# Keeping the written order of the matmuls in a hybrid encoder block's projections and second MLP product

## The chip, the cores and the metric

The kernel runs on one core of a Trainium2 chip. The metric is device time in microseconds (us) of one execution, lower is better. Three timed executions before the change took 2259.14, 2265.67 and 2268.3 us, so the median is 2265.67 us. One further execution was recorded by the hardware profiler. It took 2259.7 us, with a span from first to last instruction of 2257.9 us.

PE is the matrix engine (PEld its loading of the stationary operand), DVE, ACT and POOL are the vector, scalar and GpSimd engines, and SP issues the DMAs. PSUM is the memory into which PE accumulates, cut into banks of 128 x 512 float32.

## The reference

One layer on 2048 tokens, model width 1024, float32, one sequence:

```
mod = SiLU(c) W_ada + b_ada            -> shift, scale, gate for mixer and MLP
h   = RMSNorm(x) * (1 + scale) + shift
[xin | B | C | q | k | v | g] = h W_in           # 1024 -> 7 x 512
conv part  = B * causal_depthwise_conv3(C * xin)
retention  = chunked decay retention on rotary q, k, with v; per-head norm; SiLU(g) gate
x = x + gate  * RMSNorm(concat(conv, retention) W_out)
h = RMSNorm(x) * (1 + scale') + shift'
x = x + gate' * RMSNorm(relu(h W_1)^2 W_2)       # 1024 -> 4096 -> 1024
```

## The kernel before, in words

**A product in three parts.** Every float32 operand of the large products is split into a high and a low part (`hi`, `lo`) of a type that PE reads in one pass. ACT writes the high part, DVE the low part. The helper `mm3` then issues three matmuls into one PSUM bank: stationary high with moving high (line 141), stationary high with moving low (line 142), stationary low with moving high (line 143). The first two have the same stationary operand. All three are 128 x 128 by 128 x 512.

**The mixer.** The tokens go through in four blocks of 512. A block runs seven projections of `W_in` and two halves of `W_out`, as `gemm_nat` (tokens stationary, weights moving) or `gemm_t` (weights stationary, tokens moving). Each takes four banks, one for each 128 tokens or columns, and walks over eight steps of the inner dimension, at each step over the four banks, at each bank over the three parts. The weights come in groups of two steps through `wgroup`: one DMA of 512 KB into `raw`, an ACT copy to `whi` (line 135), a DVE subtraction to `wlo` (line 137), each with three buffers. The order of projections in a block is V, K, G, Q, XIN, then the retention (small products of 128 x 128 and 128 x 512 on the tiles `m`), CG, BG, the two halves of `W_out`. In block 0, V and three of the four banks of K are done in the start-up stage by calls of their own.

**Banks.** The pool `gp` has six banks for the names `g`, taken in turn; the pool `mp` has two for the names `m`. A projection's bank comes free when the engine that reads it is done with the projection that had the same bank six allocations earlier. For K and Q that reader is `rotary` on DVE (lines 529 and 538), which needs the tables of sines and cosines that `rope_tables` makes at the start of each block by a long row of small DVE operations (lines 361 to 397) and three ACT operations (lines 394 to 399).

**Between blocks** `h2_prep` transposes the finished block through the two `m` banks (line 480), with ACT and DVE reading them in turns (lines 484 to 486).

**The MLP.** Both products go by a scheme of seven products in place of eight on 2 x 2 blocks, for two halves B of the tokens. `fc1` has weights stationary (`wh`, `wl` from the pool `hp`) and prepared tokens moving (`qh`, `ql`). These tokens lie in the pools `hA` and `hB`, and for product number 4 in the tiles of the pool `tp`. Product 4 is the last of the seven of a step, except in the very first step. `fc2` walks, for each of the seven products, over 16 steps: it loads the step's stationary block from DRAM into the halves of a tile `f` (pool `late`, names `f`), the moving one into `wh`, `wl`, and calls `mm3` for four banks. The last six steps of the very last product are held in the pool `hB` first and then done bank by bank (`prod_held`).

**What sets the order.** The kernel is written as one program. A scheduler gives each engine its queue: it walks the program with a model of the instructions' times, and puts next on an engine what its model says can start first. The order of a queue is then fixed, and each engine works its queue in that order, waiting on semaphores for operands and free buffers. Between matmuls that accumulate into one bank with the flags of `mm3` the first must lead and the last must close; between banks nothing holds the written order.

Of the kernel before, what the change touches and what calls it, by code (L numbers as in the profile page):

```python
# [54 lines left out]
def block_kernel(  # L55
# [5 lines left out]
    nc = tc.nc  # L61
# [15 lines left out]
    def nm(s):  # L77
        n_of[s] = n_of.get(s, 0) + 1
        return f"{s}_{n_of[s]}"
# [13 lines left out]
    def bank(shape=(P, 512)):  # L93
        return gp.tile(list(shape), F32, tag="g", name=nm("g"))

    def mbank(shape=(P, 512)):
        return mp.tile(list(shape), F32, tag="m", name=nm("m"))
# [32 lines left out]
    def wgroup(src, eng=None, pool=None):  # L130
        pool, n = (wp, 3) if pool is None else (pool, 2)
        raw = pool.tile([P, 1024], F32, tag="raw", name=nm("raw"), bufs=n)
        nc.sync.dma_start(raw, src)
        hi = pool.tile([P, 1024], F32R, tag="whi", name=nm("whi"), bufs=n)
        nc.scalar.copy(hi, raw)  # L135
        lo = pool.tile([P, 1024], F32R, tag="wlo", name=nm("wlo"), bufs=n)
        (eng or nc.vector).tensor_tensor(lo, raw, hi.bitcast(F32), op=ALU.subtract)  # L137
        return hi, lo

    def mm3(ps, ah, al, bh, bl, first, last):  # L140
        nc.tensor.matmul(ps, ah, bh, start=first, stop=False)  # L141
        nc.tensor.matmul(ps, ah, bl, start=False, stop=False)  # L142
        nc.tensor.matmul(ps, al, bh, start=False, stop=last)  # L143

    ALL = list(range(NT))

    def gemm_nat(groups, lhs, ks, toks=ALL):

        bs = [bank() for _ in toks]
        n = 0  # L150
        for g, kp in zip(groups, ks):
            hi, lo = wgroup(g)
            for kk, k in enumerate(kp):
                c = slice(kk * 512, kk * 512 + 512)
                xh, xl = lhs[k]
                for ps, t in zip(bs, toks):
                    s = slice(t * P, t * P + P)
                    mm3(ps, xh[:, s], xl[:, s], hi[:, c], lo[:, c], n == 0, n == 2 * len(ks) - 1)
                n += 1
        return bs  # L160

    def gemm_t(groups, rhs):

        bs = [bank() for _ in range(4)]
        n = 0
        for kp, g in enumerate(groups):
            hi, lo = wgroup(g)
            for kk in range(2):
                k = 2 * kp + kk
                xh, xl = rhs[k]  # L170
                for j in range(4):
                    s = slice(kk * 512 + j * P, kk * 512 + j * P + P)
                    mm3(bs[j], hi[:, s], lo[:, s], xh, xl, n == 0, n == 2 * len(groups) - 1)
                n += 1
        return bs

# [10 lines left out]
    def mod1(kt):  # L187

        pt = st.tile([P, 256], F32, tag="pt", name=nm("pt"), bufs=4)
        for i in range(2):  # L190
            raw = st.tile([P, 4, 256], F32, tag="ada", name=nm("ada"), bufs=8)
            last = nc.sync.dma_start(raw, ada1[kt, i].rearrange("p (k c) -> p k c", k=4))
            for k in range(4):
                c_ = sc[:, 4 * i + k : 4 * i + k + 1]
                if i == k == 0:
                    nc.vector.tensor_scalar(pt, raw[:, k, :], c_, None, op0=ALU.mult)
                else:
                    nc.vector.scalar_tensor_tensor(  # L198
                        pt, raw[:, k, :], c_, pt, op0=ALU.mult, op1=ALU.add
                    )  # L200
        return pt, last
# [69 lines left out]
    with tc.tile_pool(name="st", bufs=NK) as st:  # L271
# [10 lines left out]
        ps = mbank()  # L282
# [28 lines left out]
        nxt, last = mod1(1)  # L311
        h0_tile(0, pts)
        start_ps = [bank() for _ in range(6)] + [extra]
        for k in range(NK):
            if k % 2 == 0 and k > 0:
                ws = startup_weights(k // 2)
            pts = nxt
            if k + 2 < NK:
                nxt, last = mod1(k + 2)
            c = slice(k % 2 * 512, k % 2 * 512 + 512)  # L320
            xh, xl = h_cur[k]
            for i, (w, t) in enumerate([(0, t) for t in range(NT)] + [(1, t) for t in range(3)]):
                if i == 2 and k + 1 < NK:
                    h0_tile(k + 1, pts)
                s = slice(t * P, t * P + P)
                hi, lo = ws[w]
                mm3(start_ps[i], xh[:, s], xl[:, s], hi[:, c], lo[:, c], k == 0, k == NK - 1)
# [5 lines left out]
    def at(tag, shape=(P, 512), dt=F32, bufs=4):  # L333
        pool = {"yh": pl, "yl": pl, "kT": late, "sg": late}.get(tag, pa)
        return pool.tile(list(shape), dt, tag=tag, name=nm(tag), bufs=bufs)
# [156 lines left out]
    NP = DFF // P // 2  # L492
# [21 lines left out]
    with pa_stack:  # L514
# [30 lines left out]
        for b in range(NB):  # L545

            if b == 0:
                vps, kps = start_ps[:NT], start_ps[NT:]
            else:
                vps = gemm_nat(w_in(VV), h_cur, KS)  # L550
# [22 lines left out]
            if b == 0:  # L573
                for t in range(3):
                    k_end(t, kps[t])
                k_end(3, gemm_nat(w_in(KK), h_cur, KS, ALL[3:])[0])
            else:
                for t, ps in enumerate(gemm_nat(w_in(KK), h_cur, KS)):
                    k_end(t, ps)
# [23 lines left out]
            for j, ps in enumerate(gemm_t(w_in(XIN), h_cur)):  # L603
                u = at("u", (P, TB + 2))
                nc.scalar.copy(u[:, 2:], ps)
                us.append(u)
# [11 lines left out]
            for t in range(NT):  # L618
                ps = mbank()
                for h in range(H):  # L620
                    s = slice(h * P, h * P + P)
# [4 lines left out]
                if b * NT + t < SEQ // P - 1:  # L626
                    ps = mbank()
                    for h in range(H):
                        s = slice(h * P, h * P + P)
# [4 lines left out]
                    else:  # L634
                        for h in range(H):
                            s = slice(h * P, h * P + P)
# [4 lines left out]
                for h in range(H):  # L641
                    s = slice(h * P, h * P + P)
# [21 lines left out]
            for j, ps in enumerate(gemm_t(w_in(CG), h_cur)):  # L664
                u = us[j]
                nc.vector.tensor_tensor(u[:, 2:], ps, u[:, 2:], op=ALU.mult)
                nc.gpsimd.tensor_copy(u[:, 0:2], halo[:, j, :])
                nc.gpsimd.tensor_copy(halo[:, j, :], u[:, TB : TB + 2])
                c_ = at("qT")
                nc.gpsimd.tensor_scalar(c_, u[:, 0:TB], cw[:, 0, j : j + 1], 1.0, op0=ALU.mult, op1=ALU.mult)  # L670
                for i in (1, 2):
                    nc.vector.scalar_tensor_tensor(
                        c_, u[:, i : i + TB], cw[:, i, j : j + 1], c_, op0=ALU.mult, op1=ALU.add
                    )
                cc.append(c_)
# [3 lines left out]
            for t in range(NT):  # L679
# [5 lines left out]
                for h in range(H):  # L685
                    s = slice(h * P, h * P + P)
# [10 lines left out]
            for j, ps in enumerate(gemm_t(w_in(BG), h_cur)):  # L697
                y = tmp()
                nc.vector.tensor_tensor(y, ps, cc[j], op=ALU.mult)
                nc.scalar.copy(yh[j], y)  # L700
                nc.vector.tensor_tensor(yl[j], y, yh[j].bitcast(F32), op=ALU.subtract)
# [9 lines left out]
            for ch, tag in enumerate(("kT", "sg")):  # L711
                ms = []
                for t, ps in enumerate(gemm_nat([wout[ch * 4 + k0 // 2] for k0, _ in ko], ys, ko)):
                    m = at(tag)
# [235 lines left out]
    def fc2(B, beside=None):  # L950
# [6 lines left out]
        def operands(i, t, pool=None):  # L957
            return split512(ld(fd[B][i][t]), held(pool) if pool else f_pair()) + split512(
                ld(right(i, t)), held(pool) if pool else w_
            )  # L960

        def prod(i, bs, upto=NP, aside=None):
            for t in range(upto):
                if beside is not None and i in (1, 2) and t % 4 == 2:
                    next(beside, None)
                ah, al, bh, bl = operands(i, t)
                for n, ps in enumerate(bs):
                    s = slice(n * P, n * P + P)
                    mm3(ps, ah[:, s], al[:, s], bh, bl, t == 0, t == NP - 1)
                if aside is not None:  # L970
                    next(aside, None)

# [35 lines left out]
        def whole(i, n):  # L1008
            prod(i, sets[n % 2])
            return sets[n % 2]  # L1010
# [36 lines left out]
        if B == 0:  # L1047
            prod(4, sets[0], NP, up)

            def lower():  # L1050
                for t in R:
                    last(t, nc.gpsimd)
                yield
                for t in R:
                    finish(1, t, (c21[t], c22[t]))
                    yield

            return lower()
        prod(4, sets[0], NP - 6, up)
        for t in prod_held(4, sets[0], NP - 6):  # L1060
            last(t, nc.vector)
# [94 lines left out]
```

## Time and profile before

| what | value |
|---|---|
| three timed executions | 2259.14, 2265.67, 2268.3 us |
| the profiled execution, its span | 2259.7 us, 2257.9 us |
| PE, PEld busy | 2162.3 us (96%), 1770.0 us (78%), 9736 instructions each |
| DVE, ACT, POOL busy | 1441.0, 981.0, 614.0 us |
| mean granted PE clock | 0.988 of full |
| start-up stage and first weights | up to about 88 us |
| mixer, four blocks | about 88 to 977 us |
| fc1, fc2 of the first half of the tokens | about 978 to 1300 us, 1300 to 1627 us |
| fc1, fc2 of the second half | about 1627 to 1932 us, 1932 to 2247 us |

A row of the timeline gives the start, the length, the engine, the line, the operation, the written tile, the read tiles (for a matmul the moving one, then the stationary one), the shape, the count, and in brackets the engine's idle time before it with what ended it. A matmul's length is that of its way through the array, and the next one starts before it ends; what a matmul costs is therefore the distance from its start to the next one's, called its pitch here. A row of the windows gives a stretch in us, its length, the busy time of PE with the matmuls that touch it, the granted clock, and DMA share and GB/s.

### The profile page before, as it was taken

The page shows a single profiled execution, that of the slowest core. Times are in us where ns is not written, and L with a number is a line of the kernel's source. Part 1 is how long each engine was busy: PE and PEld are TensorE (multiplying, and loading weights), DVE is VectorE, ACT ScalarE, POOL GpSimd, SP SyncE. Part 2 cuts the span into 40 slices and gives each one's busy share as a digit, 9 for nine tenths or more (in the row PEclk, how much of TensorE's full clock was granted, in tenths as well). Part 3 has the DMA queues.
Part 4 walks back from the last instruction along what each step waited for, and adds up shares of the span by engine and source line. Part 5 has one row for each costly group of instructions (what it writes and reads, how often), then busy time and mean ns, then how long its engine had stood idle before and what let it go on. Part 6 is the DMA issues. An engine that isn't in the chain of part 4 may idle for free.

```text
span 2257.9 us, 28832 instructions
## 1 busy us (share of the span) xinstructions
PE 2162.3 (96%) x9736; PEld 1770.0 (78%) x9736; DVE 1441.0 (64%) x2182; ACT 981.0 (43%) x1714; POOL 614.0 (27%) x457
## 2 busy tenths in 40 slices
PE   3999999999999999989999999999999999999997
PEld 3788777878777888868888877888788888888886
DVE  7766854774576535796666686555776666555557
ACT  3332532254224522565555555444455555444444
POOL 4133163305323442152333232001433333010012
PEclk8999999999999999999999999999999999999999
DMA  7456576446555563665444575666664444756556
GB/s 280 140 168 222 160 242 230 164 156 219 196 181 193 195 228 108 225 198 182 150 153 151 193 236 183 200 187 187 223 215 149 154 149 150 225 177 199 187 187 242
DMA packets 197429, 428.25 MB, mean 190 GB/s; under 512 B 22560, under 2 KB 22560, under 8 KB 197280
## 3 DMA queue, kind: packets, MB, share of 16 engines
q1 hardware_dynamic: 197280, 426.41, 56.8%
q8 instruction: 76, 1.25, 0.2%
q14 instruction: 73, 0.60, 0.1%
HBM read 322.51 MB, written 103.81 MB: 189 GB/s over the span
## 4 chain that ended last, share of the span: by engine, by line
PE 67%; issue 10%; DMA 9%; DVE 9%; POOL 3%; ACT 1%; SPq 0%; POOLq 0%; DVEq 0%; ACTq 0%
PE g L142 20%; PE g L143 20%; PE g L141 19%; DMA w2r<-in_w 2%; DMA w2d<-w2r 2%; PE m L142 2%; PE m L143 2%; PE m L141 2%; POOL w2r L501 2%; DMA ada<-in_ada 2%; DVE wlo L137 1%; DMA x<-in_x 1%; DVE wl L802 1%; DVE ql L802 1%; DVE pt L198 1%
## 5 line engine op out<-in xcount | busy, mean ns | idle before, releaser
L801 ACT CAST wh<-r 128x512 fp32r<-128x512 f32 x442 | 273.3, 618 | 220.3 <-PE g L142 203.5
L143 PE MATMUL g<-qh,wl 128*128 128x512 f32 x896 | 350.5, 392 | 7.6 <-DVE wl L802 7.6
L141 PE MATMUL g<-qh,wh 128*128 128x512 f32 x896 | 350.3, 391 | 1.8 <-ACT wh L801 1.8
L142 PE MATMUL g<-ql,wh 128*128 128x512 f32 x896 | 350.1, 391 | 0.0
L802 DVE TENSOR_TENSOR wl<-r,wh 128x512 fp32r<-128x512 f32 x442 | 321.1, 727 | 8.8 <-ACT wh L801 8.4
L802 DVE TENSOR_TENSOR f<-r,f 128x512 fp32r<-128x512 f32 x218 | 164.2, 753 | 229.0 <-ACT f L801 228.8
L135 ACT CAST whi<-raw 128x1024 fp32r<-128x1024 f32 x148 | 155.1, 1052 | 344.6 <-PE g L143 178.3
L860 DVE TENSOR_TENSOR q<-g,q 128x512 f32<-128x512 f32 x267 | 178.3, 686 | 185.6 <-PE g L143 183.3
L137 DVE TENSOR_TENSOR wlo<-raw,whi 128x1024 fp32r<-128x1024 f32 x140 | 188.1, 1347 | 149.2 <-ACT whi L135 148.8
L142 PE MATMUL g<-wl,f 128*128 128x512 f32 x680 | 271.1, 399 | 9.0 <-DVE wl L802 9.0
L801 ACT CAST f<-r 128x512 fp32r<-128x512 f32 x218 | 135.2, 620 | 311.3 <-PE m L143 149.5
L143 PE MATMUL g<-wh,f 128*128 128x512 f32 x680 | 268.5, 395 | 0.0
L143 PEld LDWEIGHTS g<-qh,wl 128*128 128x128 f32 x896 | 168.6, 188 | 44.7 <-DVE wl L802 9.0
L141 PEld LDWEIGHTS g<-qh,wh 128*128 128x128 f32 x896 | 168.6, 188 | 38.0 <-ACT wh L801 2.4
L141 PE MATMUL g<-wh,f 128*128 128x512 f32 x680 | 195.8, 396 | 1.3 <-ACT wh L801 1.3
L142 PEld LDWEIGHTS g<-ql,wh 128*128 128x128 f32 x896 | 168.6, 188 | 36.0
L987 POOL TENSOR_TENSOR q<-q,gg 128x512 f32<-128x512 f32 x28 | 42.0, 1523 | 484.9 <-ACT q L984 484.9
L142 PEld LDWEIGHTS g<-wl,f 128*128 128x128 f32 x680 | 128.5, 189 | 43.7 <-DVE wl L802 12.4
L878 POOL TENSOR_TENSOR r<-r,r 128x512 f32<-128x512 f32 x32 | 41.9, 1310 | 435.2 <-DVE wl L802 392.2
L141 PEld LDWEIGHTS g<-wh,f 128*128 128x128 f32 x680 | 128.3, 189 | 32.5 <-ACT wh L801 2.1
L143 PEld LDWEIGHTS g<-wh,f 128*128 128x128 f32 x680 | 128.5, 189 | 29.3
L141 PE MATMUL g<-whi,r 128*128 128x512 f32 x315 | 125.9, 405 | 12.5 <-DVE tmp L538 7.6
(253 smaller groups left out, 4218.5 us busy)
## 6 DMA issues: line engine op xcount, KB each, us to landing
raw<-in_win SPq DMA_DIRECT2D x116, 512.0 KB, 4.2
r<-in_w SPq DMA_DIRECT2D x224, 256.0 KB, 4.5
fd<-q SPq DMA_DIRECT2D x224, 256.0 KB, 2.2
r<-fd SPq DMA_DIRECT2D x224, 256.0 KB, 2.7
r<-w2d SPq DMA_DIRECT2D x128, 256.0 KB, 2.7
ada<-in_ada SPq DMA_DIRECT2D x48, 512.0 KB, 4.6
w2r<-in_w SPq DMA_DIRECT2D x32, 512.0 KB, 5.2
raw<-in_wout SPq DMA_DIRECT2D x32, 512.0 KB, 4.4
```

The costliest lines, as they stand in the source:

```text
L135: nc.scalar.copy(hi, raw)
L137: (eng or nc.vector).tensor_tensor(lo, raw, hi.bitcast(F32), op=ALU.subtract)
L141: nc.tensor.matmul(ps, ah, bh, start=first, stop=False)
L142: nc.tensor.matmul(ps, ah, bl, start=False, stop=False)
L143: nc.tensor.matmul(ps, al, bh, start=False, stop=last)
L198: nc.vector.scalar_tensor_tensor(pt, raw[:, k, :], c_, pt, op0=ALU.mult, op1=ALU.add)
L501: nc.gpsimd.tensor_tensor(o, a, b_, op=ALU.subtract)
L801: nc.scalar.copy(hi, src)
L802: nc.vector.tensor_tensor(lo, src, hi.bitcast(F32), op=SUB)
L860: (eng or nc.vector).tensor_tensor(o, a, b_, op=ADD)
L878: nc.gpsimd.tensor_tensor(b11, b12, b11, op=SUB)
L987: eng.tensor_tensor(c, c, gg[1][:, j * 512 : j * 512 + 512], op=ALU.mult)
```

## The change

`mm3` gets a name of a row. Matmuls that carry the same name are tied one behind the other, in the order in which they are written, by an ordering rule for the scheduler that adds no semaphore. Each projection (`gemm_nat`, and `gemm_t` in the same way as the diff shows for `gemm_nat`) is a row of its own, and all of `fc2` of one half of the tokens is one row, without the held last steps. The matmuls of the start-up stage and of `fc1` get no row. Two rows are free against each other, and so are all other instructions. No instruction is added or removed. Behind the change the three matmuls stand in lines 159 to 161, and other lines 20 further down.

```diff
+    def behind(a, b):
+        tc.add_manual_dep(
+            a.ins, b.ins.name,
+            mybir.DependencyInfo(mybir.DependencyClass.NoSync, mybir.DependencyReason.DATA),
+            reason="order",
+        )
+    row_of = {}
+    def in_row(row, m):
+        if row is not None:
+            if row in row_of:
+                behind(m, row_of[row])
+            row_of[row] = m
-    def mm3(ps, ah, al, bh, bl, first, last):
-        nc.tensor.matmul(ps, ah, bh, start=first, stop=False)
-        nc.tensor.matmul(ps, ah, bl, start=False, stop=False)
-        nc.tensor.matmul(ps, al, bh, start=False, stop=last)
+    def mm3(ps, ah, al, bh, bl, first, last, row=None):
+        in_row(row, nc.tensor.matmul(ps, ah, bh, start=first, stop=False))
+        in_row(row, nc.tensor.matmul(ps, ah, bl, start=False, stop=False))
+        in_row(row, nc.tensor.matmul(ps, al, bh, start=False, stop=last))
...
     def gemm_nat(groups, lhs, ks, toks=ALL):
         bs = [bank() for _ in toks]
+        row = nm("row")
...
-                    mm3(ps, xh[:, s], xl[:, s], hi[:, c], lo[:, c], n == 0, n == 2 * len(ks) - 1)
+                    mm3(ps, xh[:, s], xl[:, s], hi[:, c], lo[:, c], n == 0, n == 2 * len(ks) - 1, row)
...
-                    mm3(ps, ah[:, s], al[:, s], bh, bl, t == 0, t == NP - 1)
+                    mm3(ps, ah[:, s], al[:, s], bh, bl, t == 0, t == NP - 1, f"fc2_{B}")
```

The scheduler's result is shown at three places of PE's queue. A name's number tells one buffer from another: in `g_852<-whi_855,r_217` the bank is `g_852`, the moving operand `whi_855`, the stationary one `r_217`.

The first place is the third projection of block 0, G, on the banks `g_849` to `g_852`. Before, the first matmul of the fourth bank stands here:

```order
L141 MATMUL g_851<-whi_915,wh_457 128x512
L142 MATMUL g_851<-wlo_917,wh_457 128x512
L143 MATMUL g_851<-whi_915,wl_460 128x512
L141 MATMUL g_852<-whi_855,r_217 128x512
L142 MATMUL g_852<-wlo_857,r_217 128x512
L143 MATMUL g_852<-whi_855,r_220 128x512
```

It is behind the sixth of the other three banks' eight steps (`wh_457` is the sixth). Now it stands here:

```order
L159 MATMUL g_851<-whi_855,r_217 128x512
L160 MATMUL g_851<-wlo_857,r_217 128x512
L161 MATMUL g_851<-whi_855,r_220 128x512
L159 MATMUL g_852<-whi_855,r_217 128x512
L160 MATMUL g_852<-wlo_857,r_217 128x512
L161 MATMUL g_852<-whi_855,r_220 128x512
L159 MATMUL g_849<-whi_855,r_253 128x512
```

Five steps of the three other banks, 5 x 3 x 3 = 45 matmuls, stood ahead of the first matmul of `g_852` and stand behind it now.

The second place is G of block 1, on the banks `g_2723` to `g_2726`; block 2 has the same at `g_4680`. Before:

```order
L141 MATMUL g_2724<-whi_2759,r_2122 128x512
L142 MATMUL g_2724<-wlo_2761,r_2122 128x512
L141 MATMUL g_2725<-whi_2729,r_2102 128x512
L142 MATMUL g_2725<-wlo_2731,r_2102 128x512
L143 MATMUL g_2725<-whi_2729,r_2104 128x512
L141 MATMUL g_2725<-whi_2729,r_2112 128x512
L142 MATMUL g_2725<-wlo_2731,r_2112 128x512
L143 MATMUL g_2725<-whi_2729,r_2114 128x512
L143 MATMUL g_2724<-whi_2759,r_2124 128x512
L141 MATMUL g_2725<-whi_2759,r_2122 128x512
L142 MATMUL g_2725<-wlo_2761,r_2122 128x512
L141 MATMUL g_2726<-whi_2729,r_2102 128x512
```

The fourth bank comes in when the other three have gone on to the third step (`r_2122`). Now:

```order
L159 MATMUL g_2725<-whi_2729,r_2102 128x512
L160 MATMUL g_2725<-wlo_2731,r_2102 128x512
L161 MATMUL g_2725<-whi_2729,r_2104 128x512
L159 MATMUL g_2726<-whi_2729,r_2102 128x512
L160 MATMUL g_2726<-wlo_2731,r_2102 128x512
L161 MATMUL g_2726<-whi_2729,r_2104 128x512
L159 MATMUL g_2723<-whi_2729,r_2112 128x512
```

17 matmuls of the second and third inner step of the other three banks have moved from ahead of the first matmul of `g_2726` to behind it.

The third place is one step of `fc2`. Before:

```order
L141 MATMUL g_11255<-wh_12267,f_12262 128x512
L141 MATMUL g_11256<-wh_12267,f_12262 128x512
L141 MATMUL g_11257<-wh_12267,f_12262 128x512
L141 MATMUL g_11258<-wh_12267,f_12262 128x512
L142 MATMUL g_11255<-wl_12268,f_12262 128x512
L143 MATMUL g_11255<-wh_12267,f_12262 128x512
L142 MATMUL g_11256<-wl_12268,f_12262 128x512
L143 MATMUL g_11256<-wh_12267,f_12262 128x512
```

The four high-high matmuls of a step stand together, ahead of the pairs with a low part. Now:

```order
L159 MATMUL g_11255<-wh_12267,f_12262 128x512
L160 MATMUL g_11255<-wl_12268,f_12262 128x512
L161 MATMUL g_11255<-wh_12267,f_12262 128x512
L159 MATMUL g_11256<-wh_12267,f_12262 128x512
L160 MATMUL g_11256<-wl_12268,f_12262 128x512
L161 MATMUL g_11256<-wh_12267,f_12262 128x512
```

The second and third part of each bank have moved up behind its first, so that the three stand side by side, as they do in `fc1` before and after the change. At the change of block, 18 matmuls of the first half of `W_out` (two banks, three inner steps) that stood ahead of the last transposes of `h2_prep` and of the third bank's first matmul (`g_3891` in block 1, with `g_5843` and `g_7720` in blocks 2 and 3) now stand behind it.

More of the change, by code (lines that the diff above doesn't have):

```diff
@@ L164, in gemm_t @@
         bs = [bank() for _ in range(4)]
+        row = nm("row")
         n = 0
@@ L172, in gemm_t @@
                     s = slice(kk * 512 + j * P, kk * 512 + j * P + P)
-                    mm3(bs[j], hi[:, s], lo[:, s], xh, xl, n == 0, n == 2 * len(groups) - 1)
+                    mm3(bs[j], hi[:, s], lo[:, s], xh, xl, n == 0, n == 2 * len(groups) - 1, row)
                 n += 1
```

## The prediction

> **What bounds the kernel now.** I read the page first, its busy times:
>
> ```profile
> PE 2162.3 (96%) x9736; PEld 1770.0 (78%) x9736; DVE 1441.0 (64%) x2182; ACT 981.0 (43%) x1714; POOL 614.0 (27%) x457
> ```
>
> PE is busy 96% of the span, so the time is the number of matmuls times their pitch, plus what PE stands idle. The change adds and removes no matmul. It can work on two things: the pitch, and PE's idle time. The windows of stages show both: the mixer, a stretch of `fc1`, two of `fc2`.
>
> ```profile
> 130.00:930.00 800.00, 774.57 (x3738) 0.99 0.57 191
> 1780.50:1795.90 15.40, 15.40 (x69) 1.00 0.43 157
> 1400.00:1500.00 100.00, 100.00 (x432) 1.00 0.59 189
> 2020.00:2150.00 130.00, 130.00 (x559) 1.00 0.60 189
> ```
>
> In the mixer PE is idle 800 - 774.57 = 25.4 us, which is all that a better order could win there. In `fc1`, in the written order, the pitch is 15.40 / 68 = 0.2265 us (one matmul off, since those at both edges are counted). In `fc2`, in the scheduler's order, it is 100 / 431 = 0.2320 and 130 / 558 = 0.2330 us. These 6 ns are what the change could win in `fc2`, so the first question is whether the order makes them.
>
> **The pitch: order or operands?** The timeline has two stretches in which order and pitch come apart. The first is product 4 of `fc1`, the last of its step: its three parts stand side by side, but its moving operand lies in the pool `tp`, not in `hA` or `hB`. It begins at 1795.92.
>
> ```profile
> 1795.24 0.39 PE L141 MATMUL g<-qh,wh 128*128 128x512 f32 x1
> ...
> 1795.92 0.40 PE L141 MATMUL g<-qh,wh 128*128 128x512 f32 x1
> ...
> 1798.71 0.39 PE L141 MATMUL g<-qh,wh 128*128 128x512 f32 x1
> ```
>
> The last three matmuls of product 3 take 0.68 us, 0.227 each; the twelve of product 4 take 2.79 us, 0.2325 each. The slow pitch comes in the written order too. The second stretch is the held end of `fc2`, whose operands lie in `hB`:
>
> ```profile
> 2231.84 0.39 PE L143 MATMUL g<-qh,ql 128*128 128x512 f32 x1
> 2232.06 0.39 PE L141 MATMUL g<-qh,qh 128*128 128x512 f32 x1
> 2232.29 0.39 PE L142 MATMUL g<-ql,qh 128*128 128x512 f32 x1
> 2232.52 0.61 PE L141 MATMUL g<-qh,qh 128*128 128x512 f32 x2
> 2232.97 0.39 PE L143 MATMUL g<-qh,ql 128*128 128x512 f32 x1
> 2233.20 0.39 PE L142 MATMUL g<-ql,qh 128*128 128x512 f32 x1
> 2233.42 0.39 PE L143 MATMUL g<-qh,ql 128*128 128x512 f32 x1
> 2233.65 0.39 PE L142 MATMUL g<-ql,qh 128*128 128x512 f32 x1
> ```
>
> Here the parts are mixed, and the pitch is still (2233.65 - 2231.84) / 8 = 0.226 us. So the slow pitch goes with operands in the pools `late` (the tiles `f`) and `tp`, not with the order. The change moves no operand, and I cost its effect on the pitch at nothing. How many matmuls are in question is shown by the groups of `fc2`'s second part, those with `g` banks and those with `m` banks; the second row of these two is also the view of waits on low parts that part E needs:
>
> ```profile
> L142 PE MATMUL m<-wl,f 128*128 128x512 f32 x192 | 76.0, 396 | 0.0
> L142 PE MATMUL g<-wl,f 128*128 128x512 f32 x680 | 271.1, 399 | 9.0 <-DVE wl L802 9.0
> ```
>
> 3 x (680 + 192) = 2616 matmuls. The bounds of the term are 0 and 2616 x (0.2325 - 0.2265) = -15.7 us; I take 0, the row of product 4 being the nearest one.
>
> **Part A: the fourth bank of G in block 0.** At the first place where PE's queue changes, the timelines of PE and DVE show:
>
> ```profile
> 106.93 0.39 PE L143 MATMUL g<-whi,wl 128*128 128x512 f32 x1
> 109.31 0.47 PE L141 MATMUL g<-whi,r 128*128 128x512 f32 x1 [1.99 <-DVE tmp L538]
> ...
> 113.26 0.39 PE L142 MATMUL g<-wlo,r 128*128 128x512 f32 x1
> ```
>
> ```profile
> 99.53 4.56 DVE L384 SCALAR_TENSOR_TENSOR wide<-wide 128x256 f32<-128x256 f32 x10
> ...
> 107.81 0.69 DVE L529 TENSOR_TENSOR tmp<-g,coss 128x512 f32<-128x512 f32 x1 [0.57 <-ACT coss L399]
> 108.42 0.75 DVE L538 TENSOR_TENSOR tmp<-g,sins 128x256 f32<-128x256 f32 x2
> ```
>
> 109.31 is the first matmul of the fourth bank. It waits for line 538, the rotary of the K bank that lay there before. DVE is deep in the tables of sines until then and frees the bank at 108.42 + 0.75 = 109.2. Up to that point its queue is the same after the change, and nothing in it is fed by the 45 matmuls that now stand behind the wait. So PE arrives 45 x 0.227 = 10.2 us earlier, at about 97, and stands until 109.3: +10.2 us, and everything that PE feeds comes later by that. The first ten matmuls behind the wait take 113.26 - 109.31 = 3.95 us in place of 2.27: PE's clock has dropped. This price, 1.7 us, is paid already and stays.
>
> The Trainium skill ("TensorE: Matmul & The Clock Gate", "Step-by-step: what each phase is for") says that matmuls stay in program order and that only weight loads are pulled ahead. The trace agrees: PE stood 1.99 us at 109.31 with other matmuls queued behind. If PE could pass over a waiting matmul, part A would be 0 in place of 10.2.
>
> **Parts B and C: the fourth bank of G in blocks 1 and 2.**
>
> ```profile
> 334.32 0.47 PE L141 MATMUL g<-whi,r 128*128 128x512 f32 x1 [3.79 <-DVE tmp L538]
> ...
> 569.93 0.47 PE L141 MATMUL g<-whi,r 128*128 128x512 f32 x1 [1.78 <-DVE tmp L538]
> 570.24 0.40 PE L142 MATMUL g<-wlo,r 128*128 128x512 f32 x1
> 570.47 0.39 PE L143 MATMUL g<-whi,r 128*128 128x512 f32 x1
> ```
>
> The same wait stands here already, and 17 matmuls move behind it in each: 17 x 0.227 = +3.9 us each. B's wait grows from 3.8 to 7.7. C's grows from 1.8, behind which the clock was full (570.24 to 570.47 is 0.23), to 5.7, so I add the clock's 1.7 of part A. B and C: 3.9 + 3.9 + 1.7 = +9.5 us. Bounds: 0, if a late PE finds the bank free, and 11.2, if B's drop lasts longer by as much again.
>
> The skill has a rule on that clock (same page, "What's actually happening": half rate after at least one idle window of about 3.4 us, the windows running free). By it C's wait drops the clock and A's 1.99 us need not have. The row of A says that it did, so the price stands on the row.
>
> **Part D: the change of block, three times.** 18 matmuls that filled PE among the transposes move behind them:
>
> ```profile
> 475.01 1.23 PE L480 MATMUL m<-ident,vb 128*128 128x128 f32 x8 [0.30 <-DVE tmp L486]
> 476.57 1.19 PE L480 MATMUL m<-ident,vb 128*128 128x128 f32 x8 [0.33 <-DVE tmp L486]
> 478.73 0.50 PE L141 MATMUL g<-whi,yh 128*128 128x512 f32 x1 [0.97 <-DVE tmp L699]
> ```
>
> The transposes go at the pace at which the two `m` banks are read, and the last matmul shown waits for the reader of BG (line 699). If both keep their times, PE is 18 x 0.227 = 4.1 us more idle; if DVE comes to them earlier by as much, nothing. The idle time here is 0.30 + 0.33 + 0.97 = 1.6 us, where the cover is already gone; I take 1.0 more at each of the three: +3.0, bounds 0 and 12.3.
>
> **Part E: low parts in `fc2`.** Before, the 141s of three other banks ran while a late low part was made. Now the first 142 stands second in its step, and behind it wait the step's ten others. The waits name them:
>
> ```profile
> PE g L142 <- DVE wl L802: 9.0, 7, 2.8
> ```
>
> Seven waits, 9.0 us in all, each up to 3 x 0.2325 = 0.7 us longer: bounds 0 and +4.9. Where waits follow each other the lag is one, and it is regained where DVE is ahead (it is 64% busy): I take +1.0.
>
> **Part F: what a late PE finds done.** Behind part A stand three larger waits of blocks 0 and 1:
>
> ```profile
> 209.97 0.71 PE L630 MATMUL m<-va,vb 128*128 128x128 f32 x4 [2.75 <-DVE sg L654]
> ...
> 233.16 0.50 PE L143 MATMUL g<-whi,yl 128*128 128x512 f32 x1 [1.32 <-DVE yl L689]
> ...
> 297.82 0.50 PE L142 MATMUL g<-wlo,wh 128*128 128x512 f32 x1 [0.83 <-DVE wlo L137]
> ```
>
> 4.9 us together. The first two lie in the retention, which PE's own results feed, so they move with PE in part: I take -3.5, bounds 0 and -4.9.
>
> **The sum.** 10.2 + 9.5 + 3.0 + 1.0 - 3.5 = +20.2 us, and 0 for the pitch. On the profiled execution's 2259.7 us this makes 2279.9. That execution was 6.0 us under the median of the three timed ones; all four have a mean of 2263.2, and on that I put the forecast: 2283 us.
>
> **The rivals.** *The pitch does follow the order.* Then `fc2` gives 15.7 us back: 2283 - 15.7 = 2267. For it: all other products of `fc1` are in the written order and fast. Against it: both stretches above. Chance 0.13. The Trainium skill bears on it (same page, "Step-by-step: what each phase is for"): one loaded weight can serve many matmuls. The trace shows 9736 loads for 9736 matmuls, the pairs of `fc1` included, so a pair side by side saves no load.
>
> *PE makes it up (the other side).* One mechanism: the long waits of the mixer are ended by work that PE does not feed, so a late PE finds it done. Its place is B, C and D, with F in full; the price is 9.5 + 3.0 + 1.4 = 13.9 off, 2269, and down to 2259 if A's 10.2 come back in the same way. It decides if DVE's tables in blocks 1 and 2 start no later than before, for then A's lateness covers the 3.9 us of B. Against it: DVE's queue has weight subtractions between the tables, and their buffers are freed by PE. Chance 0.12.
>
> *All bounds go up.* D at 12.3, E at 4.9, F at 0: 9.3 + 3.9 + 3.5 = 16.7 more, up to 2300. Chance 0.12.
>
> *The forecast* has 0.60. The remaining 0.03 is the first two rivals together.
>
> **How the numbers follow.** The low end is 2265, just under the first rival and inside the second, and leaves about 0.08 below. The high end is 2298, near the third's far end. About 0.5%, 11.3 us, can be told from no change. Slower by more: 0.60 + 0.12, less 0.05 for the forecast's lower edge, 0.67. Within: that edge and the first two rivals, less their far end, 0.28. Faster: 0.05.
>
> **What would show each step.** A: one idle time of PE of about 12 us between 97 and 109, ended by line 558 (538 before). B and C: idle times near 7.7 and 5.7 us, ended by the same line, and slow matmuls behind C. Pitch: a window of 100 us in `fc2` with 432 matmuls speaks for the operands, with 441 for the order. D: more idle time at line 500. F: block 0's waits shorter. The forecast is wrong if `fc1` begins less than 8 us later than before, or if `fc2` takes 6 us less.

## The result and the profile after

The changed kernel takes 2287.78 us (median of six runs, 2282.52 to 2292.74) where the kernel before takes 2263.36 us (six runs, 2259.14 to 2268.3). That is 24.4 us slower; the ratio is 1.0106, 95% interval 1.0086 to 1.0126. Predicted were 2283 us, with a range of 2265 to 2298. The profiled execution of the changed kernel took 2287.11 us.

The page of the changed kernel, its busy times:

```profile
PE 2168.9 (95%) x9736; PEld 1776.6 (78%) x9736; DVE 1441.4 (63%) x2182; ACT 984.5 (43%) x1714; POOL 619.3 (27%) x457
```

The number of matmuls is the same, and the span has grown from 2257.9 to 2285.3 us. The windows by stage (start and end, length, busy time of PE with its matmuls, then PEld, DVE, ACT, POOL, granted clock, DMA share, GB/s) tell where:

```profile
130.00:930.00 800.00, 765.22 (x3660) 635.60 (x3659) 470.62 (x729) 274.84 (x480) 264.53 (x210) 0.99 0.56 185
1400.00:1500.00 100.00, 100.00 (x433) 81.05 (x431) 54.33 (x80) 43.48 (x80) 6.40 (x4) 1.00 0.60 189
2020.00:2150.00 130.00, 130.00 (x559) 104.57 (x558) 70.61 (x106) 55.38 (x101) 6.40 (x4) 1.00 0.60 188
```

In the mixer window PE is busy for 765.22 us and takes in 3660 matmuls, where it was 774.57 and 3738. In `fc2` nothing has moved: 433 matmuls in 100 us against 432, and 559 in 130 us as before. So the written order does not change the pitch, and the loss lies in the mixer. Some of the waits of PE in the mixer (us in total, times, longest; rows left out are marked) before the change:

```profile
PE g L141 <- DVE tmp L538: 7.6, 3, 3.8
...
PE m L630 <- DVE sg L654: 2.7, 1, 2.7
...
PE m L480 <- ACT tmp L484: 2.4, 6, 0.4
PE g L141 <- DVE tmp L699: 1.9, 3, 1.0
```

and the largest after it:

```profile
PE g L159 <- DVE tmp L558: 25.1, 5, 12.2
PE m L642 <- DVE S L657: 5.6, 2, 3.4
PE m L663 <- DVE tmp L644: 4.3, 1, 4.3
PE m L500 <- DVE tmp L506: 3.9, 8, 0.9
...
PE g L159 <- DVE tmp L719: 3.1, 3, 1.1
PE m L702 <- POOL sg L677: 3.1, 1, 3.1
```

The wait for the rotary of K (line 558, before 538) has grown by 17.5 us. Its three large places, in the timeline of PE:

```profile
97.01 0.39 PE L161 MATMUL g<-whi,r 128*128 128x512 f32 x1
109.64 0.77 PE L159 MATMUL g<-whi,r 128*128 128x512 f32 x1 [12.24 <-DVE tmp L558]
110.21 0.63 PE L160 MATMUL g<-wlo,r 128*128 128x512 f32 x1
110.64 0.63 PE L161 MATMUL g<-whi,r 128*128 128x512 f32 x1
...
345.82 0.77 PE L159 MATMUL g<-whi,r 128*128 128x512 f32 x1 [5.34 <-DVE tmp L558]
...
580.30 0.77 PE L159 MATMUL g<-whi,r 128*128 128x512 f32 x1 [5.88 <-DVE tmp L558]
580.87 0.63 PE L160 MATMUL g<-wlo,r 128*128 128x512 f32 x1
581.30 0.63 PE L161 MATMUL g<-whi,r 128*128 128x512 f32 x1
```

In block 0 PE now stands from about 97 to 109.6. Behind the third wait the matmuls come 0.43 us apart (580.87, 581.30): the clock is down there too, as it was not before.

How the delay builds up can be read from the last matmul of each projection, after less before, in the two timelines (us):

| end of | block 0 | block 1 | block 2 | block 3 |
|---|---|---|---|---|
| G | +9.7 | +15.3 | +14.9 | +20.9 |
| XIN | +12.5 | +10.5 | +16.6 | +23.7 |
| BG | +15.8 | +9.8 | +22.0 | +23.7 |
| second half of W_out | +13.9 | +9.3 | +19.1 | +26.4 |

It is not one step that stays. Block 0 loses 14, block 1 gives back 5, and blocks 2 and 3 lose 17 more. From there to the end the delay stays at 26 to 28.

### The profile page after: what moved, and what is told of

The parts are those of the page before. It is cut to its first block, busy times and chain, and to the rows that moved or that the text cites. A ratio compares the mean times of both kernels' runs of the same rounds, so it can differ in the third digit from the quotient of the medians.

```text
span 2285.3 us, 28815 instructions
## 1 busy us (share of the span) xinstructions
PE 2168.9 (95%) x9736; PEld 1776.6 (78%) x9736; DVE 1441.4 (63%) x2182; ACT 984.5 (43%) x1714; POOL 619.3 (27%) x457
## 4 chain that ended last, share of the span: by engine, by line
PE 70%; issue 11%; DMA 8%; DVE 6%; POOL 4%; ACT 1%; SPq 0%; POOLq 0%; DVEq 0%; ACTq 0%
PE g L159 20%; PE g L160 20%; PE g L161 20%; DMA w2r<-in_w 3%; PE m L159 2%; PE m L160 2%; PE m L161 2%; POOL w2r L521 2%; DMA w2d<-w2r 2%; DMA x<-in_x 1%; DVE pt L218 1%; POOL sg L761 1%; DVE wl L822 1%; DMA q<-h2d 1%; PE m L642 0%
## 5 line engine op out<-in xcount | busy, mean ns | idle before, releaser
L822 DVE TENSOR_TENSOR wl<-r,wh 128x512 fp32r<-128x512 f32 x442 | 326.8, 740 | 7.0 <-ACT wh L821 6.6
L822 DVE TENSOR_TENSOR f<-r,f 128x512 fp32r<-128x512 f32 x218 | 159.5, 732 | 220.0 <-ACT f L821 219.9
L159 PE MATMUL g<-wh,f 128*128 128x512 f32 x680 | 269.8, 397 | 0.8 <-ACT wh L821 0.8
L161 PE MATMUL g<-wh,f 128*128 128x512 f32 x680 | 270.1, 397 | 0.0
```

The lines of the kernel that those rows point to most:

```text
L159: in_row(row, nc.tensor.matmul(ps, ah, bh, start=first, stop=False))
L161: in_row(row, nc.tensor.matmul(ps, al, bh, start=False, stop=last))
L822: nc.vector.tensor_tensor(lo, src, hi.bitcast(F32), op=SUB)
```

## Experiments: where the loss comes from

The time of a run is a median, its ratio is against runs of the kernel before that were made in the same series (their medians lie between 2261.2 and 2265.1 us), and the interval is of 95%.

**Rows in `fc2` alone.** Edit: the projections call `mm3` without a row.

```diff
-  mm3(ps, xh[:, s], xl[:, s], hi[:, c], lo[:, c], n == 0, n == 2 * len(ks) - 1, row)
+  mm3(ps, xh[:, s], xl[:, s], hi[:, c], lo[:, c], n == 0, n == 2 * len(ks) - 1)
```

(and the same in `gemm_t`).

> The change without the rows of the projections: only fc2 keeps the written order. My theory (the whole loss lies in the mixer, order does not set the pitch): 2263 us, within 3 us of before, 432 matmuls in 100 us of fc2. Pitch by order: 2263 - 15.7 = 2248 us. Term E at its upper bound: 2268 us.

Measured: 2261.88 us, ratio 0.9991 (0.9977 to 1.0005). The windows of this run:

```profile
1380.00:1480.00 100.00, 100.00 (x431) 80.44 (x430) 53.95 (x80) 43.60 (x80) 6.39 (x4) 1.00 0.61 190
2000.00:2130.00 130.00, 130.00 (x559) 104.59 (x558) 69.72 (x105) 55.81 (x102) 6.39 (x4) 1.00 0.62 189
```

The order of `fc2` neither costs nor wins anything that can be measured. The rival in which the pitch follows the order is out, and so is the upper bound of term E.

**The fourth bank of G apart.** Edit: in the changed kernel the fourth bank of G, in each block, gets a row of its own. The banks still keep the order of their own matmuls.

```diff
-  def gemm_nat(groups, lhs, ks, toks=ALL):
+  def gemm_nat(groups, lhs, ks, toks=ALL, apart=()):
...
-  mm3(..., n == 2 * len(ks) - 1, row)
+  mm3(..., n == 2 * len(ks) - 1, row + "b" if t in apart else row)
...
-  for ps in gemm_nat(w_in(GG), h_cur, KS):
+  for ps in gemm_nat(w_in(GG), h_cur, KS, ALL, (3,)):
```

> The change, but the fourth bank of G has a row of its own in each block, so that it may come later than the other three. Terms A to C carry the loss: the waits for line 558 fall from 25.1 to about 7.6 us and 1.7 us of slow clock go, 2288 - 19 = 2269 us. PE makes it up in part (block 1 gave back 4 us of what block 0 lost): only about half of that is won, 2278 us. The loss comes from elsewhere in the rows: 2288 us.

Measured: 2275.79 us, ratio 1.0057 (1.0039 to 1.0076). The waits of PE in its mixer:

```profile
PE g L159 <- DVE tmp L558: 7.1, 5, 2.5
PE m L663 <- DVE tmp L644: 4.1, 1, 4.1
PE m L500 <- DVE tmp L506: 3.9, 8, 0.9
PE m L642 <- DVE S L657: 3.7, 2, 3.3
```

The wait for line 558 is back at 7.1 us, as my terms A to C have it, but the time above the kernel before falls by 10.9 us (24.4 to 13.5), not by 19. So 18 us of waiting that can be seen in a trace were worth 11 us of time, and 13.5 us come from other rows.

**Part A alone.** Edit: the kernel before with one row, that of G in block 0 (`gemm_nat(w_in(GG), h_cur, KS, tied=b == 0)`, no row anywhere else).

> The kernel before with one row only, that of projection G in block 0: part A alone. If A's delay stays to the end, as my sum has it: 2262.3 + 10.2 = 2272.5 us. If a late PE finds the next waits done (the wait of 3.8 us in block 1 and the 3.1 us at 396 of before): 2262.3 + 10.2 - 3.8 - 3.1 = 2265.6 us, and the delay against before falls from 10 at the end of G in block 0 to 3 to 4 us at the end of block 1.

Measured: 2272.93 us, ratio 1.0038 (1.0025 to 1.0051), 9.5 us above before. The delay was 10.9 us at the end of G in block 0, 12.5 at the end of block 1 and 10.2 at the end of the mixer. Its waits for line 558:

```profile
PE g L159 <- DVE tmp L558: 17.1, 3, 13.2
```

and its timeline at the fourth bank of G in block 1:

```profile
345.06 0.47 PE L159 MATMUL g<-whi,r 128*128 128x512 f32 x1 [1.88 <-DVE tmp L558]
```

Part A stays to the end. The wait in block 1 was covered only in part: the bank came free at about 345.06 us in place of 334.32, and PE still waited for 1.88 us in place of 3.79. The 2 us won there were lost again in XIN of the same block (delay 10.5 us at the end of G, 12.5 at the end of XIN). The rival "PE makes it up" is out for A, as far as it rests on A's 10 us. What the run with the fourth bank apart won beyond it, 10.9 - 9.5 = 1.4 us, is what B and C are worth in time by these medians; the intervals leave this difference uncertain by some 7 us.

**Which rows make the other 13.5 us?** Two halves, without rows in `fc2`: rows only on the projections with the weights stationary (XIN, CG, BG), and rows only on the others (V, K, G with its fourth bank apart, Q, W_out).

```diff
-  mm3(bs[j], hi[:, s], lo[:, s], xh, xl, n == 0, n == 2 * len(groups) - 1, row)
+  mm3(bs[j], hi[:, s], lo[:, s], xh, xl, n == 0, n == 2 * len(groups) - 1)
```

(this makes the second half; the first takes `row` out of `gemm_nat` in the same way).

> Rows only on the projections with the weights stationary (XIN, CG, BG). The run with the fourth bank of G apart left 13 us of loss, first seen around the retention of block 2 (5 us) and in XIN of block 3 (4 us). If these rows make it, because their matmuls filled PE in the retention: 2274 us. If it is the rows of the other projections (V, K, Q, W_out): 2263 us.

> The other half: rows only on the projections with the tokens stationary (V, K, G, Q, W_out), the fourth bank of G apart. If the rows of XIN, CG and BG make the rest of the loss: 2263 us. If these do: 2274 us. If it is neither alone, both lie in between, and the sum of both losses is near 13 us.

Measured: XIN, CG and BG 2266.62 us, ratio 1.0012 (1.0000 to 1.0024); the others 2270.34 us, ratio 1.0028 (1.0017 to 1.0038). Neither alone: +3.2 and +7.0 us, 10.2 together. In the trace of the second run the delay grows by 6.1 us at the first half of W_out in block 0 and by 3.2 in block 2. In the whole mixer it has these waits at the transposes of the retention's result:

```profile
PE m L702 <- POOL sg L677: 4.9, 2, 2.7
PE m L702 <- DVE sg L674: 2.2, 1, 2.2
```

In block 0 stands one of them, of 2.1 us, the others in block 2; from 228 to 266 us the granted clock is 0.91, where it was 1.00 before (228 to 260 us). Before, the same waits (its line 682) were 1.7 and 0.7 us, both in block 2. W_out takes the four groups of 128 tokens as four banks, and the token groups' operands come out of the retention one after the other. This led to the next run.

**Rows on W_out alone.** Edit: `tied=True` for the two halves of W_out, no other row.

> Rows only on the two halves of W_out in each block. In the trace of the run with rows on V, K, G, Q and W_out, the delay against before grew by 6.1 us at the first half of W_out in block 0 and by 3.2 in block 2, with new waits at the transposes of line 702. If W_out's rows are the rest of the loss of that run: 2263.4 + 7 = 2270 us. If it comes from the rows of V, K and Q: 2263 us.

Measured: 2273.52 us, ratio 1.0050 (1.0037 to 1.0062), 12.3 us above before. That is more than both halves of the pair before, so the effects of rows do not simply add. This run varied more than others (2267.08 to 2276.69), and its profile is of the fastest of its executions, in which the mixer ended only 4.4 us late. The two fastest executions had a granted clock of 0.987 and 0.988, the other eight of 0.982 to 0.986. Where in the program the slower ones lose the rest is not on record.

**Each bank of W_out apart as well.** Edit: the run with the fourth bank of G apart, and in addition a row for each bank of W_out.

```diff
-  row + "b" if t in apart else row)
+  f"{row}_{t}" if t in apart else row)
...
-  gemm_nat([wout[ch * 4 + k0 // 2] for k0, _ in ko], ys, ko)
+  gemm_nat([wout[ch * 4 + k0 // 2] for k0, _ in ko], ys, ko, ALL, ALL)
```

> The change, with the fourth bank of G in a row of its own and each bank of the two halves of W_out in a row of its own; within a bank the three parts keep their order, and V, K, Q, XIN, CG, BG and fc2 keep their rows over all banks. If the loss is that a row over several banks stops at the bank that is late (G's fourth, and W_out's banks of the tokens transposed last): the 13 us that the run with G's fourth bank apart still lost go too, but for the 3 us of XIN, CG and BG: 2265 us. If it is the order of the parts within a bank that costs in W_out: 2275 us as with G's fourth bank apart alone.

Measured: 2267.62 us, ratio 1.0009 (0.9996 to 1.0022), 2.5 us above before. With the order kept inside each bank, and across banks everywhere but at these two places, the loss is gone to within what can be measured. This holds the main result: taken apart in this order, the 24.4 us are 10.9 at the fourth bank of G (24.4 to 13.5), 11.0 at the banks of W_out (13.5 to 2.5), and 2.5 for all other rows together. By the intervals the first two are uncertain by some 5 to 6 us each, and the third cannot be told from nothing; since the effects of rows do not simply add, another order could share the sum out otherwise. It is not the order of the three parts that costs, but the tie between banks at these two places.

How the tie costs time, the traces show for G alone. These are the windows of the mixer, from 88 us to the first matmul of `fc1`, in the kernel before, in the changed kernel, in the run with the fourth bank of G apart, and in this run:

```profile
88.00:978.50 890.50, 859.67 (x4121) 711.62 (x4120) 560.84 (x873) 322.50 (x569) 292.45 (x229) 0.99 0.57 191
88.00:1004.90 916.90, 863.54 (x4122) 716.51 (x4121) 564.76 (x873) 324.06 (x569) 296.98 (x229) 0.98 0.56 186
88.00:990.10 902.10, 867.15 (x4122) 718.00 (x4121) 565.38 (x873) 323.15 (x569) 289.85 (x229) 0.98 0.57 189
88.00:985.80 897.80, 858.94 (x4118) 711.25 (x4119) 566.50 (x873) 321.76 (x569) 295.48 (x229) 0.99 0.57 190
```

Length less busy time is PE's idle time: 30.8, 53.4, 35.0 and 38.9 us. Letting the fourth bank of G go takes 18.4 us of idle time out, nearly all of it at line 558: a row over four banks stops there as a whole at the bank that is late. The time falls by less because PE is busy for 3.6 us more with the same matmuls, and the MLP takes 3.1 us longer. Letting the banks of W_out go takes no idle time out. What falls is the busy time, by 8.2 us, with the granted clock at 0.99 in place of 0.98, and the clock differs between executions of the same queues too. So that the rows of W_out cost time is shown by the medians; that they do it by stopping at a late bank is not shown, and where the 11.0 us are paid stays open.

## Experiments: what sets the pitch

The prediction put the slow pitch of `fc2` and of product 4 down to the pool in which an operand lies, without saying why. The pools start at these bytes of a partition: `late` at 23936 and `tp` at 56704, `hp` at 77568, `wp` and `hB` at 110336, `pl` at 147200, `hA` at 179968. The first two are 128 past a multiple of 256, all others are on one, and the tiles are whole multiples of 2048 bytes. Each slow matmul has one operand in `late` or `tp` and the other in `hp`. Two runs move the pools; for this, four columns of constants get a tile and a DMA of their own. The queues of PE, DVE and ACT are those of before.

**`late` and `tp` on multiples of 256.** Edit:

```diff
-    border = keep.tile([P, 16], F32, name="border")
+    border = keep.tile([P, 40], F32, name="border")
...
-        cst_sb = tp.tile([P, 1120], F32, tag="cst", name="cst_sb", bufs=1)
-        nc.sync.dma_start(cst_sb[:, 0:1092], cst)
+        cst_sb = tp.tile([P, 1088], F32, tag="cst", name="cst_sb", bufs=1)
+        nc.sync.dma_start(cst_sb, cst[:, 0:1088])
+        kdec = keep.tile([P, 4], F32, name="kdec")
+        nc.sync.dma_start(kdec, cst[:, 1088:1092])
```

> The kernel before, with the same queues on PE, DVE and ACT, but with the tiles of the pools late and tp 128 bytes further up, so that they start on multiples of 256 bytes as those of all other pools do. Four columns of constants move to a tile of their own to make room. If the start address modulo 256 makes the slow pitch: a window of 100 us in fc2 shows about 441 matmuls in place of 432, product 4 of fc1 has the pitch 0.227, and the time is 2263.4 - (2616 + 384) x 0.0058 = 2246 us. If the low half of the memory is slow wherever a tile starts: 432 and 2263 us. If the order of the matmuls makes it: 432 and 2263 us.

**Everything behind them off by 128.** Edit: the same, with `border` of 8 columns, so that `late` and `tp` stay and the pools behind them move down by 128 bytes.

> The kernel before with late and tp where they were, and all pools behind them 128 bytes further down, so that no operand starts on a multiple of 256 bytes. If an operand's own start address matters: the other 8832 - 3000 = 5832 large matmuls take 0.2325 too, +34 us, 2297 us, a window of 100 us in fc1 shows 432 in place of 441. If it is the difference between the start addresses of the two operands of a matmul that matters: none differ modulo 256 now, fc2 shows 441, 2246 us. If the part of the memory or the order matters: no change, 2263 us.

Measured: 2247.39 us, ratio 0.9939 (0.9916 to 0.9961), and 2245.74 us, ratio 0.9922 (0.9901 to 0.9943). Both are faster than before, and equal within their intervals. The windows of the first run, in `fc1` and `fc2`:

```profile
1100.00:1200.00 100.00, 100.00 (x443) 82.83 (x442) 63.98 (x95) 50.33 (x83) 30.40 (x20) 1.00 0.43 145
1380.00:1480.00 100.00, 100.00 (x443) 82.84 (x442) 56.32 (x82) 43.97 (x82) 6.41 (x4) 1.00 0.62 193
2000.00:2130.00 130.00, 130.00 (x575) 107.66 (x574) 72.51 (x109) 56.71 (x104) 6.41 (x4) 1.00 0.62 193
```

and of the second:

```profile
1100.00:1200.00 100.00, 100.00 (x443) 82.78 (x442) 63.85 (x94) 50.57 (x83) 30.40 (x20) 1.00 0.46 148
1380.00:1480.00 100.00, 100.00 (x443) 82.81 (x442) 56.52 (x82) 44.28 (x82) 6.41 (x4) 1.00 0.62 194
2000.00:2130.00 130.00, 130.00 (x575) 107.67 (x574) 72.99 (x108) 56.61 (x104) 6.41 (x4) 1.00 0.62 193
```

443 matmuls in 100 us is a pitch of 0.2262 us everywhere. In the second run no operand starts on a multiple of 256, and all matmuls are fast. So it is not an operand's own start that counts, and not the half of the memory, but how the starts of a matmul's two operands stand to each other: alike modulo 256 they are fast, 128 apart they took 0.2328 in place of 0.2268 (means over some 2,580 matmuls of `fc2`).

**Other distances.** Edit: the kernel before with `late` 64 and `tp` 96 bytes further up.

```diff
-    border = keep.tile([P, 16], F32, name="border")
+    border = keep.tile([P, 32], F32, name="border")
...
+    gap = ctx.enter_context(tc.tile_pool(name="gap", bufs=1))
+    gap_t = gap.tile([P, 8], F32, name="gap_t")
     tp = ctx.enter_context(tc.tile_pool(name="tp", bufs=8))
...
-        cst_sb = tp.tile([P, 1120], F32, tag="cst", name="cst_sb", bufs=1)
+        cst_sb = tp.tile([P, 1096], F32, tag="cst", name="cst_sb", bufs=1)
```

> The kernel before with the pool late 64 and the pool tp 96 bytes further up: fc2's stationary operands start 192 past a multiple of 256 bytes, product 4's moving operands 224, and the other operands of both on a multiple. If any difference modulo 256 makes the slow pitch: 432 matmuls in 100 us of fc2, 0.2325 us in product 4, 2262 us. If only a difference of 128 does: 442, 2246 us. If it grows with the distance from the next multiple: fc2 in between, about 436, product 4 nearer to 0.227, 2254 us.

Measured: 2255.31 us, ratio 0.9963 (0.9950 to 0.9976). Its windows in the two halves of `fc2`:

```profile
1380.00:1480.00 100.00, 100.00 (x430) 81.00 (x429) 54.51 (x79) 42.94 (x80) 6.44 (x4) 1.00 0.60 187
2000.00:2130.00 130.00, 130.00 (x569) 106.66 (x569) 71.74 (x107) 56.63 (x104) 6.45 (x4) 1.00 0.61 192
```

The time fits the third theory, but its reasons don't hold: with the same distance of 192 the pitch is 100 / 429 = 0.2331 in the first window and 130 / 568 = 0.2289 in the second, and product 4, 224 past a multiple and so only 32 short of one, takes 0.2335 (mean of 383). None of the three theories holds as it stands. What the runs show is that equal starts modulo 256 are fast and that three other distances are slow, by 2 to 7 ns. How much a distance costs, and why it differs between stretches with the same distance, stays open.

**The change on aligned memory.** Edit: the changed kernel with the pools of the first of these runs.

> The whole change, with the tiles of late and tp on multiples of 256 bytes as in the first experiment. If order and pitch have nothing to do with each other, both effects add: 2287.8 - 16 = 2272 us, with 442 matmuls in 100 us of fc2. If the written order has an effect on the pitch that the start addresses hid: below 2268 us, with more than 443 matmuls.

Measured: 2269.75 us, ratio 1.0034 (1.0023 to 1.0046), with 443 matmuls in 100 us of `fc2`. The two effects add: 24.4 - 14.9 = 9.5 was to be expected from the medians, and 8.6 came.

## Why the prediction was right, and where it wasn't

The direction, the size and the range held: +20.2 us were forecast and +24.4 measured. By its steps:

- **What bounds the kernel, and the pitch at 0: right.** 433 matmuls against 432 in `fc2`, and with rows in `fc2` alone a ratio of 0.9991. The two short stretches of the old trace in which order and operands come apart were enough to tell. The first rival (0.13) is out.
- **Part A, +10.2: right.** In the changed kernel the wait grew from 1.99 to 12.24 us, and the row of G in block 0 alone cost 9.5 us.
- **Parts B and C, +9.5: too high in time.** The waits themselves came nearly as forecast: C from 1.78 to 5.88 us with the clock down behind it, B from 3.79 to only 5.34. But in time the two are worth 1.4 us (10.9 for A to C together, less 9.5), a difference of medians that the intervals leave uncertain by some 7 us. In the changed kernel XIN and CG of block 1 gave back 15.3 - 9.0 = 6.3 us (9.0 is the delay at the end of CG). The 1.5 us of them in CG come in the run with the fourth bank of G apart as well; the 4.8 in XIN don't. In XIN of the old trace stands a wait that I had not put into part F:

```profile
PE g L141 <- ACT whi L135: 2.9, 1, 2.9
```

  It is gone after the change: the copy that PE waited for began at 405.65 us in place of 394.94, 10.7 us later, and PE came later still. With part A alone the copy began at 407.09 us, 12.2 later, and PE still waited for 3.2 us. So the mechanism of the second rival, a late PE that finds the work done, is seen here in one place, behind B's wait in the changed kernel; it did not touch A.
- **Part D, +3.0: right at its place, but the rows of W_out cost more.** At the changes of block the waits of lines 500 and 719 (480 and 699 before) grew from 4.9 to 7.6 us, by 2.7. By the medians, though, letting the banks of W_out go won 11.0 us. The step that failed is that a row over the four banks of W_out was priced only by the 18 matmuls at the transposes of `h2_prep`; the other 8 us have no term in the sum. In the run with rows on V, K, G, Q and W_out a part of it stands in block 0, where there is no `h2_prep`. In the changed kernel the delay does not grow there (15.8 us at the end of BG, 14.8 at the end of the first half of W_out), so the place of the 8 us stays open.
- **Part E, +1.0: right.** The waits of the second part for its low operand fell from 9.0 to 7.3 us, and the run with rows in `fc2` alone shows nothing.
- **Part F, -3.5: wrong in place.** The waits of PE in the mixer other than those of parts A to D (lines 538, 699 and 480 before) did not fall: they add up to 18.2 us before and 20.7 after, because new ones came into the retention (line 642, 5.6 us, and line 663, 4.3 us). The run with rows on XIN, CG and BG alone has the same two (5.3 and 3.9 us), so they come with the rows of these projections, for which the sum had no term; that run is only 3.2 us slower than before. What was gained is the 6.3 us in block 1.

So by the medians B and C were about 8 us too high and the rows of W_out 8 us dearer than D, and the total came out near by two errors of opposite sign. That nearness is luck; what the forecast had right is the direction, part A and the pitch. The third rival (all bounds up, 2300 us) is nearer in what the rows of W_out cost, though it too looked for it at the transposes of `h2_prep`.

The rule of the Trainium skill ("TensorE: Matmul & The Clock Gate", "Step-by-step: what each phase is for") that the prediction weighed, matmuls stay in program order, is borne out: PE stood for 12.24 us, to 109.64, with 45 matmuls queued behind the late bank that the kernel before had all started by 106.93.

The version that beats both kernels is the kernel before with its pools moved: 2245.74 us for the second placing, 2247.39 for the first, against 2262.33 us. It needs no order at all.

## What to carry to other kernels

An ordering rule over several accumulators can turn one late accumulator into a stop of the whole engine, as at the fourth bank of G: tie the order within an accumulator, where the experiments found next to no cost, and leave accumulators free against each other where their banks or operands come at different times. Look for a slow pitch by comparing matmuls with the same shape and different operand tiles in one trace before any order is changed; here 128 bytes of padding were worth 15 us, and the written order in `fc2` nothing that could be measured. And a wait that is seen in a trace is not yet its worth in time: 18 us of waits at one line were worth 11, while PE worked more slowly elsewhere.

## What the runs showed of the hardware that was not expected

- **Two operands of a matmul and their start addresses.** Equal starts modulo 256 gave 0.2268 us a matmul in `fc2`, starts 128 apart 0.2328, 192 apart 0.2289 or 0.2331, 224 apart 0.2335 (product 4). Whether both started on a multiple of 256 or both 128 past one made no difference. This was measured with this one type and shape.
- **The clock drops after idle times from about 2 us, and not always after the same.** The wait of 1.99 us at the fourth bank of G in block 0 dropped it in the kernel before. In the run with the banks of G and W_out apart a longer one at the same place did not:

```profile
109.13 0.47 PE L159 MATMUL g<-whi,r 128*128 128x512 f32 x1 [2.52 <-DVE tmp L558]
109.44 0.40 PE L160 MATMUL g<-wlo,r 128*128 128x512 f32 x1
109.67 0.40 PE L161 MATMUL g<-whi,r 128*128 128x512 f32 x1
```

  Over all traces the shortest idle time that stands alone and is followed, about 1 us on, by large matmuls 0.43 us apart is 1.91 us (the run with other distances, at 566.6 us), and the longest followed by large matmuls at full speed is 3.17 us (rows in `fc2` alone, at 1363.6 us). That is as if idleness were judged in fixed stretches: one of them has to lie whole in the idle time, which is never so below its length and always so above twice its length. By the two ends its length would be between 3.17 / 2 = 1.6 and 1.9 us, an estimate. The Trainium skill ("TensorE: Matmul & The Clock Gate", "What's actually happening") has free-running windows of about 3.4 us; that they run free agrees, their length here does not.
- **The same queues vary from run to run by more than the differences in question.** Rows on W_out alone gave 2267.08 to 2276.69 us in ten runs, with granted clocks of 0.988 down to 0.982; one profile shows one of these.
